# Opening with filler products, another order of transfers, block 1 plain; the last 24 modulation column tiles moved out of the raw ring

## The chip, the cores and the metric

The kernel runs on one core of one Trainium2 chip. The time is device microseconds (us) of that core for one launch. The kernel before takes 1838.76 us (median of 3 runs, 1837.59 to 1839.71). The engines are named PE (matrix products; PEld its weight loads), DVE (vector), ACT (scalar), POOL (GpSimd) and SP (the sync engine, which here issues most transfers). Each engine works through its own instructions strictly in order and waits at the first one that isn't ready.

## The reference

One layer of a diffusion trunk over 640 tokens: 512 latent ones, which use the conditioning vector `c`, and 128 context ones, which use `c_ctx`. The model width is 1024, the inner width of each FFN 2816. All is float32.

```python
def adaln(cvec, w, b):
    m = jax.nn.silu(cvec) @ w + b
    return m.reshape(cvec.shape[0], N_MOD, D_MODEL)        # N_MOD = 9

def swiglu(h, w1, w3, w2):
    return (jax.nn.silu(h @ w1) * (h @ w3)) @ w2

def layer(x, mods, l, p, ctx):
    m = [mods[:, j][:, None, :] for j in range(N_MOD)]
    hh = rmsnorm(x, g[0]) * (1 + m[1]) + m[0]
    x = x + 0.5 * m[2] * swiglu(hh, p['ffn1_w1'][l], p['ffn1_w3'][l], p['ffn1_w2'][l])
    hh = rmsnorm(x, g[1]) * (1 + m[4]) + m[3]
    y, ctx_out = token_mixer(hh, p, l, ctx)
    x = x + m[5] * y
    hh = rmsnorm(x, g[2]) * (1 + m[7]) + m[6]
    x = x + 0.5 * m[8] * swiglu(hh, p['ffn2_w1'][l], p['ffn2_w3'][l], p['ffn2_w2'][l])
```

`token_mixer` is a differential attention and an mLSTM side by side; its end is `y = sigmoid(gm) * (hm @ w_br_m) + sigmoid(gd) * (att @ w_br_d)` and then `y @ w_out`. The nine vectors `m[j]` depend on the conditioning alone: 9 x 1024 values for each of two vectors, which are 72 column tiles of 128 values.

## The kernel before

**Data.** The tokens lie along the free axis in two halves of 320 (`HALF`, `hf` 0 and 1), the features in 8 tiles of 128 partitions (`KT`). Every factor of a float32 product is split into a high and a low part, and a product is the three matmuls high x high, high x low and low x high (`mm3`), each 128x128 by 128x320. So a product of 128 outputs by 320 tokens over 1024 inputs takes 24 matmuls. All of them are recorded by one helper line (L75), and copies to the high part by L51 (ACT), differences to the low part by L54 (DVE), loads by L97. In the names, `wH` and `wL`, `ww`, `wB`, `wC` are split weights, `raw` the weights as loaded, `hm` and `S` the normalised activations and their sums.

**Stages.**

1. The opening (0 to about 53 us). `x` comes in by `load_x`; `Opening.squares`, `add_squares`, `rstd` and `refine` make the norm's 1/rms (the sum over partitions is a product with `ones`, tile `ps_ss`), `divide` applies it. The modulation columns m[0] and m[1] come from `Opening.product(k)`, 16 matmuls on a 1 MB piece of `w_ada` (`raw_a`, a ring of four buffers, `load(k)`), k = 0 to 7, and `columns(k)`, a small product (`ps_at`) after a copy on DVE (`small`, L802). `norm(hf, r)` applies scale and shift. Between these stand the eight steps of the first FFN block: `step(first, k, 0)` multiplies feature tile k of half 0. After them `second` does half 1. This stage is emitted in the order in which the code is written (`as_written`).
2. FFN1, up. The inner width is cut into 11 blocks of 256. Block 0 is the one of the opening, plain. From block 2 on, and for w3 of block 1, a block is done by Winograd's form: 7 products of 12 matmuls (84) in place of 4 of 24 (96) (`Winograd.products`), for which the weights' sums are made by `Granule.parts` and `sums` (`ww`, `wB`, `wC`; split on ACT, then on DVE). w1 of block 1 is plain (`Whole`). The step counter `i` runs over w1 and w3 of the blocks, two steps a block; `between(i, at)` puts other work into a step.
3. FFN1, down; the mixing (input projections, attention, mLSTM), with `Fill` granules put between.
4. The branches: products with `w_br_d` (tiles `w_brd`), with `w_br_m` (`w_brm`) and with `w_out`, 16 units each of 24 matmuls (`ps_p`); the sigmoid gates are read back from DRAM (`sig`), and `d_evac` and `m_evac` take the results out of PSUM on DVE.
5. FFN2, up and down (`HalfStep.run`): blocks 0 to 2 with their gate plain, 3 to 10 gated on Winograd's sums. The residual `x` is read again from `x2_dram` into `x_pairs`.

**Column tiles.** The other 56 column tiles are made by `Columns.tile` (L716): one tile is a load of 512 KB (`raw_a` or `ada`) and two DVE instructions, each of which multiplies it with one conditioning vector (`csil`) and sums. 14 of them stand in FFN1 up, 18 in FFN1 down, with loads on POOL's queue. The last 24 stand in the mixing and in stage 4. Their loads (`load_columns_raw`) share a ring of two buffers (`rawp`) with the weights `w_brd`, `w_brm`, `z_raw` and are issued by SP, in one queue with those.

**What sets the order.** Outside the parts emitted as written, a scheduler orders each engine's instructions; `tc.issue_after(x)` only says after which instruction the next ones may be put. Each engine's queue is in order, and so are SP's transfers: SP waits at a transfer until its buffer is free, and everything behind it waits too.

## Time and profile before

| | us |
|---|---|
| median of 3 runs | 1838.76 |
| the profiled execution | 1840.36 |
| its span in the profile | 1838.6 |
| PE busy in it | 1799.5 |
| DVE busy | 1317.2 |
| ACT busy | 867.7 |

The profiled execution is 1.6 us above the median. PE is busy for all but 39 us of the span. Busy does not mean full speed: its instructions also last longer where the granted clock is low, and the profile gives that clock for any stretch of time. The places at which PE waits, and what ended each wait, are listed with the prediction.

### The profile page before, as it was taken

The page shows a single profiled execution, that of the slowest core. Times are in us where ns is not written, and L with a number is a line of the kernel's source. Part 1 is how long each engine was busy: PE and PEld are TensorE (multiplying, and loading weights), DVE is VectorE, ACT ScalarE, POOL GpSimd, SP SyncE. Part 2 cuts the span into 40 slices and gives each one's busy share as a digit, 9 for nine tenths or more (in the row PEclk, how much of TensorE's full clock was granted, in tenths as well). Part 3 has the DMA queues.
Part 4 walks back from the last instruction along what each step waited for, and adds up shares of the span by engine and source line. Part 5 has one row for each costly group of instructions (what it writes and reads, how often), then busy time and mean ns, then how long its engine had stood idle before and what let it go on. Part 6 is the DMA issues. An engine that isn't in the chain of part 4 may idle for free.

```text
span 1838.6 us, 30679 instructions
## 1 busy us (share of the span) xinstructions
PE 1799.5 (98%) x12608; PEld 1761.4 (96%) x12608; DVE 1317.2 (72%) x2148; ACT 867.7 (47%) x1490; POOL 31.0 (2%) x55
## 2 busy tenths in 40 slices
PE   7999999999999999999999999999899999999999
PEld 5999999999999999999999999999899999999999
DVE  5898886577787757475585558876766878887575
ACT  4654454112655555454465555673235645554232
POOL 0000001110000000000000000000000000000000
PEclk8999999999999999999999999999999999999999
DMA  7354547975234322122222154574742345447872
GB/s 289 121 192 169 193 169 250 370 239 176 72 122 145 122 81 79 63 85 67 77 77 84 41 168 147 199 268 164 257 174 86 132 149 188 166 170 254 322 286 87
DMA packets 127709, 298.77 MB, mean 162 GB/s; under 512 B 9617, under 2 KB 90769, under 8 KB 114769
## 3 DMA queue, kind: packets, MB, share of 16 engines
q1 hardware_dynamic: 118306, 256.44, 40.1%
q0 software_dynamic: 9264, 40.37, 6.0%
q8 instruction: 99, 1.62, 0.4%
q14 instruction: 40, 0.33, 0.1%
HBM read 233.15 MB, written 63.63 MB: 161 GB/s over the span
## 4 chain that ended last, share of the span: by engine, by line
PE 84%; DVE 6%; DMA 5%; ACT 3%; issue 1%; SPq 0%; DVEq 0%; ACTq 0%
PE ps_f L75 45%; PE ps_p L75 16%; PE ps_t L75 11%; PE sc L75 3%; PE ps_o L75 2%; PE ps_n L75 2%; DMA ada<-csil_dram 2%; DVE ww L54 1%; PE ps_u L75 1%; PE ps_wT L78 1%; DMA raw_a<-in_w_ada_c 1%; PE ps_qkT L78 1%; DVE raw_a L716 1%; ACT wH L51 1%; PE ps_ss L75 1%
## 5 line engine op out<-in xcount | busy, mean ns | idle before, releaser
L75 PE MATMUL ps_f<-S,ww 128*128 128x320 f32 x2172 | 350.2, 310 | 5.8 <-DVE ww L54 4.2
L75 PEld LDWEIGHTS ps_f<-S,ww 128*128 128x128 f32 x2172 | 327.0, 189 | 8.5 <-DVE ww L54 6.9
L75 PE MATMUL ps_p<-hH,wH 128*128 128x320 f32 x672 | 213.4, 318 | 6.9 <-DVE y L54 6.2
L75 PE MATMUL ps_p<-hL,wH 128*128 128x320 f32 x672 | 208.2, 310 | 0.0
L75 PE MATMUL ps_p<-hH,wL 128*128 128x320 f32 x672 | 208.2, 310 | 0.0
L51 ACT ACTIVATE ww<-raw 128x2048 fp32r<-128x2048 f32 (+1 forms) x67 | 125.6, 1874 | 154.9 <-PE ps_f L75 87.6
L75 PE MATMUL ps_f<-hm,ww 128*128 128x320 f32 x1236 | 195.6, 311 | 2.5 <-DVE ww L54 2.5
L75 PEld LDWEIGHTS ps_f<-hm,ww 128*128 128x128 f32 x1236 | 185.8, 189 | 2.8 <-DVE ww L54 2.8
L75 PE MATMUL ps_t<-wH,hH 128*128 128x256 f32 x640 | 185.3, 289 | 0.9 <-DVE x L57 0.9
L75 PE MATMUL ps_t<-wH,hL 128*128 128x256 f32 x640 | 181.1, 283 | 0.9 <-DVE hL L54 0.9
L75 PE MATMUL ps_t<-wL,hH 128*128 128x256 f32 x640 | 180.9, 283 | 0.0
L54 DVE TENSOR_TENSOR ww<-raw,ww 128x2048 fp32r<-128x2048 f32 (+1 forms) x67 | 150.1, 2240 | 38.7 <-ACT ww L51 38.7
L75 PE MATMUL ps_f<-hm,wB 128*128 128x320 f32 x984 | 157.6, 309 | 0.0
L75 PEld LDWEIGHTS ps_f<-hm,wB 128*128 128x128 f32 x984 | 147.7, 188 | 0.0
L54 DVE TENSOR_TENSOR raw<-raw 128x1024 f32<-128x1024 f32 x159 | 137.6, 865 | 2.0
L75 PEld LDWEIGHTS ps_p<-hH,wH 128*128 128x128 f32 x672 | 126.9, 189 | 7.6 <-ACT wH L51 6.4
L75 PEld LDWEIGHTS ps_p<-hL,wH 128*128 128x128 f32 x672 | 126.9, 189 | 0.3
L75 PEld LDWEIGHTS ps_p<-hH,wL 128*128 128x128 f32 x672 | 126.7, 189 | 0.0
L54 DVE TENSOR_TENSOR wL<-raw,wH 128x2048 fp32r<-128x2048 f32 x43 | 98.3, 2286 | 35.6 <-ACT wH L51 35.6
L75 PEld LDWEIGHTS ps_t<-wH,hH 128*128 128x128 f32 x640 | 122.4, 191 | 1.5 <-ACT nsq L51 1.1
L75 PEld LDWEIGHTS ps_t<-wH,hL 128*128 128x128 f32 x640 | 122.4, 191 | 1.1 <-DVE hL L54 1.1
L75 PEld LDWEIGHTS ps_t<-wL,hH 128*128 128x128 f32 x640 | 122.5, 191 | 0.4
(303 smaller groups left out, 3353.7 us busy)
## 6 DMA issues: line engine op xcount, KB each, us to landing
g_dram<-g SPq DMA_DIRECT2D x44, 640.0 KB, 5.6
raw_a<-in_w_ada_c SPq DMA_DIRECT2D x24, 512.0 KB, 4.0
raw<-in_w1b SPq DMA_DIRECT2D x11, 1024.0 KB, 4.8
raw<-in_w3b SPq DMA_DIRECT2D x11, 1024.0 KB, 4.8
raw<-in_w1a SPq DMA_DIRECT2D x10, 1024.0 KB, 4.8
raw<-in_w3a SPq DMA_DIRECT2D x10, 1024.0 KB, 6.2
ada<-in_w_ada_c POOLq DMA_DIRECT2D x18, 512.0 KB, 5.0
hm<-g_dram POOLq DMA_DIRECT2D x7, 1280.0 KB, 10.5
```

Source lines behind the costliest of these rows:

```text
L51: return placed(nc.scalar.activation(*args, **kw))
L54: return placed(eng.tensor_tensor(out=out, in0=in0, in1=in1, op=op))
L75: tc.keep_in_program_order(nc.tensor.matmul(*args, **kw))
L78: tc.keep_in_program_order(nc.tensor.transpose(*args, **kw))
L716: placed(vec.tensor_tensor_reduce(out=junk, in0=raw, in1=self.csil[:, v, :], op0=ALU.mult, op1=ALU.add, scale=1.0, scalar=0.0, accum_out=m ...
```

## The change

- **Opening.** The transfer of `cT` goes from SP to ACT's queue, so that `x` is first on SP; the first piece of w1 and w3 (`load_weights(0)`) goes ahead of `raw_a` 0, the second half of `x` behind `raw_a` 5. New products of `ones` with `ones` (`keep_clock`, 128x128 by 128x128, tile `ps_idle`, read by nobody) stand in four places: 14 + 3 + 4 + 2. The squares of half 0 are added with three matmuls in place of two, after one addition of half the size; `rstd` stands ahead of `product(0)`, whose copy moves from DVE to ACT; `divide` works on one feature tile at a time for the first two. The squares of half 1 move to k = 3, their sum to k = 4, `refine(1)` from k = 5 to 6.
- **Block 1** of FFN1 is plain for w3 too (`whole_units` twice), so the Winograd form begins with block 2.
- **`products`**: the parts of the second granule are made ahead of `ahead()` (the second batch of operand sums), not behind it.
- **Column tiles.** 10 of the 24 stay in the mixing with the ring. 6 stand in stage 4 beside `w_br_m`, and 8 in FFN2 up at every second step (i = 3, 5, ..., 17). These 14 use one pair buffer for the load and one for `junk`, both of the residual's `x_pairs` (in FFN2 the other two hold `csil`, read again), and POOL's queue. So the second half of `x_pairs` is loaded behind the six tiles, and in FFN2 the residual is read again at step 18 instead of step 0, at which the pair buffers become free.

```diff
-    cT = load(cp, [128, KT, 2], a["cT"], name="cT")
+    cT = cp.tile([128, KT, 2], F32, name="cT")
...
+    nc.scalar.dma_start(out=cT, in_=a["cT"])
...
             if ahead is not None:
                 with tc.issue_after(work[0][0].split_at):
-                    behind = ahead()
+                    work[1][0].parts(self.fp)
+                with tc.issue_after(work[1][0].parts_at):
+                    ahead()
...
+            def keep_clock(self, n):
+
+                if not hasattr(self, "idle"):
+                    self.idle = self.bank(3, "ps_idle")
+                for _ in range(n):
+                    mm(self.idle[:, :128], ones, ones, start=True, stop=True)
...
-        for r in range(2):
-            start.squares(0, r)
-            start.add_squares(0, r)
+        start.keep_clock(14)
+        start.squares(0, 0)
+        start.add_squares(0, 0)
+        start.squares(0, 1)
+        split_weights(0, "high")
+        split_weights(0, "low", slice(1))
+        start.add_squares(0, 1)
+        start.rstd(0)
+        split_weights(0, "low", slice(1, 2))
         start.product(0)
         start.load(4)
-        load_weights(3)
-        start.rstd(0)
-        split_weights(0, "high")
+        load_weights(2)
+        start.keep_clock(3)
         start.refine(0)
         start.columns(0)
-        start.divide(0, 0)
+        start.keep_clock(4)
+        start.divide(0, 0, 1)
+        start.norm(0, 0)
         start.product(1)
-        split_weights(0, "low")
-        start.norm(0, 0)
+        start.divide(0, 0, 1, 1)
         start.load(5)
+        load_x(1, 0)
+        load_x(1, 1)
+        start.keep_clock(2)
...
+        whole_units(whole[0], gated[0], ((0, 1), (1, 1), (0, 0), (1, 0)))
         with tc.issue_after(end.ins), tc.issue_after(at_act.ins):
             third, fourth = hs.operand_sums(lambda r: x_all[:, 2 * r : 2 * r + 2, :])
+        whole[1].split()
+        hs.up[3].load()
+        hs.store_g(hs.SO, 0)
+        whole_units(whole[1], gated[1], ((0, 0), (1, 0), (0, 1), (1, 1)))
...
-    columns.place(24, csil2, load_columns_raw, 1)
+    columns.place(10, csil2, load_columns_raw, 1)
...
-        if i > 1:
-            columns.tile()
...
-    while fill.q:
-        fill.units(2)
-        if columns.n > 6:
-            columns.tile()
+    fill.drain()
...
+    def load_columns_pair(src):
+        raw = pair("k", 2, "raw_a").rearrange("p a t -> p (a t)")[:, :D]
+        nc.gpsimd.dma_start(out=raw, in_=src)
+        return raw, junk
...
+    columns.place(6, csil2, load_columns_pair, 1)
...
-        for g in range(4):
+        for g in range(2):
             nc.sync.dma_start(out=x_pairs[g], in_=x_dram[:, 2 * g : 2 * g + 2, :])
...
+                if not columns.n:
+                    x_pairs += [pair("k", i, "x") for i in range(2, 4)]
...
-    def after():
-        fourth()
-        for g in range(4):
-            nc.sync.dma_start(out=x_pairs[g], in_=x2_dram[:, 2 * g : 2 * g + 2, :])
-        hs.store_g(SO, 0)
+    def aside(i, at):
+        if (i, at) == (0, 1):
+            fourth()
+            hs.store_g(SO, 0)
+        elif (i, at) == (1, 1):
...
+            columns.place(8, Two(places[:2]), load_columns_pair, 1)
+        elif at and 3 <= i < 3 + 15 and i % 2 == 1:
+            columns.tile(hs.at_vec)
+        elif (i, at) == (18, 1):
+            x_pairs[:] = pairs("k", "x")
```

**Order, PE at the opening.** The first products of the program; `ps_idle` are the fillers, `ps_ss` the sums of squares, `ps_a` the products on `raw_a`, `ps_f` the first FFN block. One piece of the difference (`-` before, `+` the change):

```order
-L75 MATMUL ps_ss<-sq,ones 128x320 x4
+L75 MATMUL ps_idle<-ones 128x128 x14
+L75 MATMUL ps_ss<-sq,ones 128x320 x6
 L75 MATMUL ps_a<-raw_a,small 32x256 x8
+L75 MATMUL ps_idle<-ones 128x128 x3
 L75 MATMUL ps_at<-sel,small 128x2 x2
+L75 MATMUL ps_idle<-ones 128x128 x4
+L75 MATMUL ps_a<-raw_a,small 32x256 x8
+L75 MATMUL ps_idle<-ones 128x128 x2
+L75 MATMUL ps_f<-hm,wH 128x320 x4
+L75 MATMUL ps_at<-sel,small 128x2 x2
```

The fillers stand ahead of the sums of squares, around the first `ps_at`, and once more ahead of the first FFN step. `product(1)` now stands ahead of that step as before, and the second `ps_at` behind its first four products.

**Order, SP at the branches.** SP's queue where `w_br_d` ends and `w_br_m` begins. Before:

```order
L97 DMA z_raw<-zT_dram 128x1920
L97 DMA raw_a<-in_w_ada_c 128x1024
L97 DMA raw<-in_w_brd 128x2048
L97 DMA raw_a<-in_w_ada_c 128x1024 x4
L97 DMA raw<-in_w_brm 128x2048 x2
L2104 DMA x<-x_dram 128x1280 x4
```

and now:

```order
L97 DMA z_raw<-zT_dram 128x1920 x2
L97 DMA sig<-gd_dram 128x1280
L97 DMA raw<-in_w_brd 128x2048
L97 DMA raw<-in_w_brm 128x2048 x3
L2146 DMA x<-x_dram 128x1280 x2
```

The five `raw_a` ahead of the first `w_br_m` are gone from this queue, three of `w_br_m` stand right behind the last `w_br_d`, and two loads of `x` have moved behind.

**Order, DVE in FFN2 up, a step with a column tile** (w3 of a gated block). `SO`, `s`, `t` are gate work on the results, `ww`, `wC`, `wB` the split of the next granule's sums. Before:

```order
L54 TENSOR_TENSOR ww<-raw,ww 128x2048
L54 TENSOR_TENSOR s<-ps_f,u 128x320
L54 TENSOR_TENSOR wC<-raw,wC 128x512
L54 TENSOR_TENSOR SO<-ps_f,s 128x320
L54 TENSOR_TENSOR wB<-raw,wB 128x1024
L54 TENSOR_TENSOR t<-ps_f,u 128x320
```

and now:

```order
L54 TENSOR_TENSOR s<-ps_f,u 128x320
L54 TENSOR_TENSOR SO<-ps_f,s 128x320
L721 ISA junk,mod<-raw_a,csil 128x1024
L721 ISA mod 128x1
L54 TENSOR_TENSOR ww<-raw,ww 128x2048
L54 TENSOR_TENSOR wC<-raw,wC 128x512
L721 ISA junk,mod<-raw_a,csil 128x1024
L721 ISA mod 128x1
L54 TENSOR_TENSOR wB<-raw,wB 128x1024
```

The first half of the tile stands ahead of `ww`, the second between `wC` and `wB`. So it is in six of the eight tiles; in the other two `ww` and `wC` stand ahead of both halves.

More of the change, by code (lines that the diff above doesn't have):

```diff
@@ L401, in products @@
                     then[i + 2 - n].load()
-                if not last:
-                    with tc.issue_after(behind if i == 0 and ahead is not None else gr.split_at):
+                if not last and (i > 0 or ahead is None):
+                    with tc.issue_after(gr.split_at):
                         work[i + 1][0].parts(self.fp)
@@ L599, in run_whole, with run @@
                     unit(G[-1], j, f, 1)
-        def run(self, x, gate, final, ahead, after):
+        def run(self, x, gate, final, ahead, aside):
             def nothing(*args):
@@ L937, in tile_trunk @@
             if k == 5:
[L938 removed]
+                whole[0].split(t=[((0, 2048, w1[0]),), ((0, 1792, w1[1]), (1792, 2048, w1[2][:, :256]))])
                 hs.up[2].load()
```

112 lines of the change are left out of this document (70 added, 42 removed).

## The prediction

> **What bounds the kernel now.** I read the page first, then the waits of PE, then windows and timelines at the places where those waits lie.
>
> ```profile
> span 1838.6 us, 30679 instructions
> ...
> PE 1799.5 (98%) x12608; PEld 1761.4 (96%) x12608; DVE 1317.2 (72%) x2148; ACT 867.7 (47%) x1490; POOL 31.0 (2%) x55
> ```
>
> PE is the bound over the whole program: 39.1 us of the span are not busy. So a microsecond can come off only in three ways: fewer products, a wait of PE that goes, or products that run at a higher clock. The view of waits says what PE waited for:
>
> ```profile
> PE ps_ss L75 <- DVE sq L54: 7.7, 1, 7.7
> PE ps_f L75 <- DVE ww L54: 6.7, 7, 2.5
> PE ps_p L75 <- DVE y L54: 6.2, 1, 6.2
> PE ps_f L75 <- ACT hm L51: 2.7, 1, 2.7
> PE ps_at L75 <- DVE small L802: 2.2, 3, 1.1
> ```
>
> The columns are us in total, times, and the longest. These five rows are 25.5 of the 39.1 us, and the change touches the place of each: the opening (`ps_ss`, `hm`, `small`), the split weights `ww` at the start of each FFN, and the one wait of 6.2 in the branches.
>
> **The opening.** Windows (us, then each engine's busy time and count, then PE's granted clock, DMA share, GB/s):
>
> ```profile
> 15.40:19.20 3.80, 1.07 (x16) 0.42 (x16) 3.14 (x8) 2.19 (x5) 0.00 (x0) 0.73 1.03 388
> 19.20:31.20 12.00, 11.95 (x64) 9.23 (x64) 5.25 (x13) 4.94 (x8) 0.00 (x0) 0.52 1.04 404
> 33.70:38.00 4.30, 3.79 (x37) 2.74 (x40) 3.48 (x9) 2.99 (x6) 0.00 (x0) 1.00 0.67 271
> 38.00:42.00 4.00, 4.00 (x35) 3.10 (x35) 2.75 (x7) 1.71 (x3) 0.00 (x0) 1.00 0.00 2
> ```
>
> From 19.2 to 31.2 PE is busy throughout at a clock of 0.52: about 5.8 us of these 12 are lost to the clock. The transfers run full until 33.7 + 0.67 x 4.3 = 36.6 and then stop. The first FFN product waits for a chain; pieces of it (start, us), and then rows of PE's timeline:
>
> ```profile
> 0.74 0.40 SPq L97
> ...
> 6.79 0.83 DVE sq L54
> ...
> 12.30 1.77 PE ps_a L75 x16
> 14.10 0.42 DVE small L802
> ...
> 17.69 0.83 DVE x L54
> ```
> ```profile
> 19.25 1.44 PE L75 MATMUL ps_f<-hm,wH 128*128 128x320 f32 x4 [2.67 <-ACT hm L51]
> ...
> 39.83 0.99 PE L75 MATMUL ps_f<-hm,wH 128*128 128x320 f32 x4
> ...
> 42.36 1.07 PE L75 MATMUL ps_a<-raw_a,small 128*32 128x256 f32 x16
> 43.37 1.34 PE L75 MATMUL ps_ss<-sq,ones 128*128 128x320 f32 x4
> 44.30 0.99 PE L75 MATMUL ps_f<-hm,wH 128*128 128x320 f32 x4
> ...
> 46.84 1.07 PE L75 MATMUL ps_a<-raw_a,small 128*32 128x256 f32 x16
> ```
>
> What the edit takes from the chain: `x` no longer stands behind `cT` on SP (0.40); `rstd` no longer behind product 0 and its copy (from 12.30 to 14.52, 2.2); one addition and one division are half as long (0.4 each of 0.83). Together 3.4, so the first step stands at 15.8 instead of 19.25. If the clock is then full, a step costs 43.37 - 39.83 = 3.54 with its `ps_a`, and the sums of squares 44.30 - 43.37 = 0.93 a piece. The last product on `raw_a` (46.84) stands behind the first step's twelve products (42.36 - 39.83 = 2.53), five steps and two sums: 15.8 + 2.5 + 17.7 + 1.9 = 37.9, which is 8.9 less. Transfers give nearly the same floor: as many bytes as before go ahead of the last `raw_a`, so it lands near 37 again, a gain of at most 9.6. At full clock the copies on DVE have less room; `ps_at` waited 2.2 in three places already, and I add two waits of about half a microsecond (estimate from 2.2 over three). I take **-8.0**, between -3.4 (the chain alone, the clock as before) and -9.6. The 14 first fillers lie in the 7.7 us in which PE has nothing. The other 9 stand ahead of the first step; a product of 128 columns costs at most the 0.27 us of a 320-column one at low clock, so 2.4 us if that cover were gone; it is the 2.67 wait for `hm`. `cT` on ACT's queue holds ACT's first instruction until it lands; behind it are the squares, which need `x` anyway.
>
> A rule on the clock bears on this. The Trainium skill (TensorE: Matmul & The Clock Gate, What's actually happening) says the clock is halved by default, becomes full after about 3.4 us of sustained activity and falls back after an idle window. The fall after the wait of 2.67 us agrees with it, the 12 us at 0.52 with PE 11.95 busy do not; by the rule alone the fillers would hold the clock, by that row a single gap near the start would cost most of the 5.8 us.
>
> **Block 1 and the starts of the Winograd parts.** PE's timeline in FFN1 and in FFN2, and one window:
>
> ```profile
> 93.69 0.56 PE L75 MATMUL ps_f<-S,ww 128*128 128x320 f32 x2 [1.30 <-ACT ww L51]
> 96.02 3.04 PE L75 MATMUL ps_f<-S,ww 128*128 128x320 f32 x10 [1.77 <-DVE ww L54]
> ```
> ```profile
> 96.00:98.90 2.90, 2.88 (x11) 2.88 (x12) 2.90 (x4) 1.47 (x2) 0.00 (x0) 0.50 0.62 220
> ```
> ```profile
> 1462.02 1.92 PE L75 MATMUL ps_f<-hm,wC 128*128 128x320 f32 x12
> 1463.78 1.92 PE L75 MATMUL ps_f<-hm,wB 128*128 128x320 f32 x12
> ...
> 1470.83 1.73 PE L75 MATMUL ps_f<-S,ww 128*128 128x320 f32 x10 [1.32 <-DVE ww L54]
> ```
>
> Twelve products take 1463.78 - 1462.02 = 1.76 us at full clock (0.147 each). A plain w3 of block 1 has 96 instead of 84: +1.76. It covers the making of the first sums: both waits go (1.30 + 1.77 = 3.07), and with them the half clock behind them (2.90 x 0.50 = 1.45). Net **-2.7**; it is +1.8 if the same wait merely moves behind block 1, where the sums now have a whole plain step (96 x 0.147 = 14.1 us) more. In FFN2 the second granule's parts now precede the operand sums: the wait of 1.32 goes, **-1.3**, at worst 0.
>
> **The branches.** SP's queue, ACT's wait, PE's timeline, a window:
>
> ```profile
> 1270.85 16.96 SPq L97 DMA_DIRECT2D raw_a<-in_w_ada_c  x4
> 1290.17 3.94 SPq L97 DMA_DIRECT2D raw<-in_w_brm  x2
> ```
> ```profile
> ACT wH L51 <- DMA raw<-in_w_brm: 19.3, 2, 18.7
> ```
> ```profile
> 1280.67 0.41 PE L75 MATMUL ps_p<-aHL,wL 128*128 128x320 f32 x1 [1.08 <-DVE wL L54]
> ...
> 1300.90 0.60 PE L75 MATMUL ps_p<-hH,wH 128*128 128x320 f32 x1 [6.19 <-DVE y L54]
> ```
> ```profile
> 1300.90:1304.10 3.20, 3.20 (x12) 3.20 (x13) 2.05 (x1) 0.00 (x0) 0.00 (x0) 0.52 1.03 424
> ```
>
> The wait of 6.19 is put down to DVE's `y`, but DVE stood behind the split of `w_brm`, whose weights were late: SP spent 16.96 us on four `raw_a`, each waiting for a ring buffer that DVE had to free, and only at 1290.17 issued `w_brm`; ACT waited 18.7 for it. In the new order three `w_brm` follow `w_brd` directly, with the whole ring to themselves. So 6.19 goes, and the slow clock behind it (12 products in 3.20 instead of 1.76: 1.44). Of the 1.08 at the last `w_brd` I count 0.4, since that split keeps its place. **-8.0**, between -8.7 and 0. The six tiles in this stage cost PE nothing as long as DVE gets them done under 16 units of 24 products, 16 x 24 x 0.147 = 56.4 us; their price if not is the rival below.
>
> **The tiles in FFN2.** A tile in FFN1 and what PE's weight load waited behind it; DVE's load in FFN2; the transfers:
>
> ```profile
> 118.94 1.22 DVE L716 CUSTOM_DVE_ANT_0 junk<-raw_a,csil 128x1024 bf16<-128x1024 f32 x1
> ...
> 122.42 0.19 PEld L75 LDWEIGHTS ps_f<-S,ww 128*128 128x128 f32 x1 [0.38 <-DVE ww L54]
> ```
> ```profile
> 1500.00:1700.00 200.00, 200.00 (x1365) 200.00 (x1365) 159.97 (x202) 103.23 (x142) 0.00 (x0) 1.00 0.54 189
> ```
> ```profile
> raw_a<-in_w_ada_c SPq DMA_DIRECT2D x24, 512.0 KB, 4.0
> ...
> ada<-in_w_ada_c POOLq DMA_DIRECT2D x18, 512.0 KB, 5.0
> hm<-g_dram POOLq DMA_DIRECT2D x7, 1280.0 KB, 10.5
> ```
>
> PE has no gap in the 200 us, DVE is at 80%. Two steps last 2 x 84 x 0.147 = 24.7 us, of which DVE is busy 19.7; a tile adds 2 x 1.22 = 2.44, so it fits on average. But half a tile stands ahead of `ww` in six of the eight, as in FFN1, where PE then waited 0.38: 6 x 0.38, **+2.3**, between 0 and 8 x 2.44 = 19.5. A tile that waits for its load holds DVE, behind it `ww` and the gate work, and PE behind those; the load has two steps to land in, against 5.0. The re-reading of the residual (640 x 1024 floats, 2.6 MB) moves to the end of the up part; at 424 GB/s that is 6.2 us of transfers beside those with which the down part begins. I take **+0.5**, between 0 and 6.2. The eight loads stand on POOL ahead of the down part's `hm`, but the last is issued before step 17.
>
> **The sum.** -8.0 - 2.7 - 1.3 - 8.0 + 2.3 + 0.5 = -17.2. The profiled execution took 1840.36, so its like would take 1823.2; it lies 1.6 above the median 1838.76, from which the forecast is **1821.6**.
>
> **The rivals.**
>
> *The clock isn't held.* For it: 12 us at 0.52 with PE busy, after one gap of 2.67; the fillers are short and stand in four groups with gaps between. Against it: the gap is what they fill. Then the opening gives -3.4: 1821.6 + 4.6 = 1826.2.
>
> *The branch wait stays* (the change doesn't do what it says there). For it: the row names DVE's `y`, and `y` needs the gates' read-back `sig`, which keeps its place. Against: ACT's 18.7 ended with the landing of `w_brm`. Then +8.0: 1829.6.
>
> *DVE becomes the bound in FFN2.* Each tile delays PE by its whole length: 19.5 - 2.3 = 17.2 more, 1838.8, no change. For it: DVE's work is uneven, and `ww` is what PE waits for 7 times. Against: 2.5 us of each 24.7 are still free.
>
> *POOL's queue is too slow for one buffer* (slower). The six tiles in the branches share one load buffer, so a tile takes its landing time plus 2.44, and in the order the sixth stands on DVE ahead of the split of the first `w_out`. 56.4 / 6 - 2.44 = 7.0: up to a landing time of 7.0 us nothing is lost, beyond it six times the excess. With 5.0 there is room; with the 10.5 that `hm` took on the same queue, 6 x 3.5 = 21 and a slow clock of 1.4 behind: 1844.0. For it: the landing on POOL's queue is already 5.0 against 4.0. The Trainium skill (SBUF — State Buffer, SBUF: two separate sides) speaks for it as well: transfers issued by GpSimd have their descriptors written by it, and some DVE instructions lock it out meanwhile. By that rule the landing grows with DVE's load; the trace's 5.0 against 4.0, with DVE busy, is a small effect of that kind.
>
> **How the numbers follow.** The forecast 64%, the clock 16%, the branch wait 8%, DVE as the bound 5%, POOL's queue 7%. The first three lie between 1814 and 1832 with their own spread: at the low end all terms at their best (-9.6 - 2.7 - 1.3 - 8.7 = -22.3, 1816.5) and two more of the waits on `ww` (6.7 in all, 3.1 of them counted); at the high end the branch wait with 2 us of the other costs. I leave the last two out, so the range is **1814 to 1832**. About 0.2% (3.7 us) is what a measurement of this kernel tells from no change. Faster: the first three, 88%; within it: DVE as the bound, 5%; slower: POOL's queue, 7%.
>
> **What would show it.** Right: PE's first FFN step before 16.5 at a clock of 1.00 and the last `ps_a` near 38; no wait over 1 us between 85 and 105; no `ps_p` wait over 1 us in the branches; in FFN2 up six short waits on `ww`. Wrong: a clock near 0.5 after the first step (the first rival); a `ps_p` wait on `y` with `sig` late; waits on `ww` of 1 us and more at steps 3, 5, ..., 17; `raw_a` on POOL landing after 7 us and more with PE waiting at the first `w_out`.

## The result, and the profile after

The kernel with the change takes 1829.17 us (median of 4 runs, 1826.73 to 1829.58) against 1838.17 us for the kernel before on the same chip (4 runs, 1836.37 to 1839.71): a ratio of 0.9944, 95% interval 0.9932 to 0.9956. It is faster by about 9 us. The forecast, 1821.6, was 7.6 us too low. Of the changed kernel, the profiled execution took 1829.16 us. Its page:

```profile
span 1827.4 us, 30792 instructions
...
PE 1802.1 (99%) x12670; PEld 1764.7 (97%) x12670; DVE 1311.0 (72%) x2141; ACT 863.2 (47%) x1486; POOL 38.4 (2%) x69
```

The span fell by 11.2, and the time in which PE isn't busy from 39.1 to 25.3 (1827.4 - 1802.1). What PE waited for now (us in total, times, the longest):

```profile
PE ps_a L75 <- DMA raw_a<-in_w_ada_k: 3.7, 2, 1.9
PE ps_f L75 <- DVE ww L54: 3.6, 3, 3.3
PE ps_f L75 <- DMA hm<-g_dram: 2.2, 1, 2.2
...
PE ps_f L75 <- ACT u L51: 0.9, 1, 0.9
...
PE ps_p L75 <- DVE y L54: 0.7, 1, 0.7
```

All five rows that the prediction shows of before are gone or small: `ps_ss` 7.7, `hm` on ACT 2.7 and `small` 2.2 no longer stand among them, `y` fell from 6.2 to 0.7, and `ww` from seven waits to three. But one of those three is 3.3 long, and a transfer that PE never waited for, `hm<-g_dram`, now costs 2.2. Where each microsecond went is read from a few products that both programs have; here are their rows in PE's timeline (start, us). Before:

```profile
67.55 0.46 PE L75 MATMUL ps_f<-hm,wgA 128*128 128x320 f32 x2
393.40 1.92 PE L75 MATMUL ps_f<-op,ww 128*128 128x320 f32 x12
1235.88 0.46 PE L75 MATMUL ps_p<-aHL,wH 128*128 128x320 f32 x2
1379.80 0.31 PE L75 MATMUL ps_p<-hH,wo 128*128 128x320 f32 x1
1695.48 1.48 PE L75 MATMUL ps_f<-S,ww 128*128 128x320 f32 x9
1706.08 1.48 PE L75 MATMUL ps_f<-S,ww 128*128 128x320 f32 x9
```

and after:

```profile
60.35 0.46 PE L75 MATMUL ps_f<-hm,wgA 128*128 128x320 f32 x2
384.80 1.92 PE L75 MATMUL ps_f<-op,ww 128*128 128x320 f32 x12
1227.91 0.46 PE L75 MATMUL ps_p<-aHL,wH 128*128 128x320 f32 x2
1363.57 0.31 PE L75 MATMUL ps_p<-hH,wo 128*128 128x320 f32 x1
1680.08 1.48 PE L75 MATMUL ps_f<-S,ww 128*128 128x320 f32 x9
1694.61 1.48 PE L75 MATMUL ps_f<-S,ww 128*128 128x320 f32 x9
```

The difference of each pair is how far the changed program is ahead there; the difference of two such differences is what the stage between them gained (negative in the table) or lost.

| stretch, up to | ahead by | change of time in it | in the forecast |
|---|---|---|---|
| opening: first gate product | 7.20 | -7.20 | -8.0 |
| FFN1: products on `op` in its down part | 8.60 | -1.40 | -2.7 |
| mixing: first `w_brd` | 7.97 | +0.63 | 0 |
| branches: first `w_out` | 16.23 | -8.26 | -8.0 |
| FFN2 up: end, at the first `S` products of its down part | 15.40 | +0.83 | -1.3 + 2.3 = +1.0 |
| FFN2: start of the down part | 11.47 | +3.93 | +0.5 |

So the gain stood at 16.2 us at the first `w_out`, against 18.7 in the forecast up to there, and almost 5 us were given back in FFN2. These are differences of one execution each; how far a stage scatters is said where it matters.

**Opening.** Windows (us; busy time and count of PE, PEld, DVE, ACT, POOL; granted clock, DMA share, GB/s), then PE's timeline:

```profile
15.40:19.20 3.80, 3.80 (x39) 2.94 (x32) 2.28 (x6) 1.78 (x4) 0.00 (x0) 1.00 1.03 407
19.20:31.20 12.00, 12.00 (x119) 9.06 (x111) 8.17 (x20) 7.10 (x12) 0.00 (x0) 1.00 1.03 398
```
```profile
16.46 0.83 PE L75 MATMUL ps_f<-hm,wH 128*128 128x320 f32 x4
...
34.64 1.07 PE L75 MATMUL ps_a<-raw_a,small 128*32 128x256 f32 x16 [1.87 <-DMA raw_a<-in_w_ada_k]
...
40.19 1.07 PE L75 MATMUL ps_a<-raw_a,small 128*32 128x256 f32 x16
```

PE does 119 products in the 12 us in which it did 64 before: the clock is 1.00 and not 0.52. The first step starts at 16.46 (19.25 before) and the last `ps_a` at 40.19 (46.84). What stops PE now is the landing of `raw_a`.

**FFN1.** In its down part DVE has a column tile that needs `csil`, read back from `csil_dram`. This row of DVE, before, then the same instruction after, and what PE did behind it:

```profile
347.83 1.23 DVE L716 CUSTOM_DVE_ANT_0 ada<-ada 128x1024 bf16<-128x1024 f32 x1 [14.14 <-DMA ada<-csil_dram]
```
```profile
339.23 1.22 DVE L721 CUSTOM_DVE_ANT_0 ada<-ada 128x1024 bf16<-128x1024 f32 x1 [5.68 <-DMA ada<-csil_dram]
...
346.51 1.91 PE L75 MATMUL ps_f<-hm,ww 128*128 128x320 f32 x7 [3.31 <-DVE ww L54]
```

The two rows are 8.60 apart, exactly the offset of the `op` products behind them. DVE stood idle until `csil` landed, `ww` stood behind the tile, and PE waited 3.31 for `ww` (2.51 before): from here on the landing sets the time, and what was gained ahead of it beyond 8.60 is lost. SP began to issue this read-back (of the second conditioning vector) at 319.69 before and at 319.79 after, behind loads of `w2a`, though PE was 9.4 ahead there; the DMA share is 1.03 and 1.04 from 320 to 340 us, so the transfers were full in both. Why it landed 8.60 earlier all the same isn't shown.

**Branches.** The first row is of PE's timeline, the second a window, the third a row of the view of transfers for 1280 to 1370 us (KB each, median us from issue to landing):

```profile
1286.06 0.38 PE L75 MATMUL ps_p<-hH,wH 128*128 128x320 f32 x1 [0.68 <-DVE y L54]
```
```profile
1284.00:1364.00 80.00, 79.33 (x541) 79.10 (x540) 56.76 (x93) 27.93 (x33) 2.67 (x6) 1.00 0.58 206
```
```profile
raw_a<-in_w_ada_c POOLq DMA_DIRECT2D x6, 512.0 KB, 5.1
```

The wait of 6.19 is 0.68, the clock behind it is 1.00, and the loads on POOL's queue land after 5.1 us, well below the 7.0 from which, by the prediction's estimate, the tiles would have held the stage up.

**The start of FFN2's down part.** PE's timeline, a window around it, and SP's queue ahead of it, in the kernel before and now:

```profile
1687.70 2.24 PE L75 MATMUL ps_f<-hm,ww 128*128 128x320 f32 x9 [2.17 <-DMA hm<-g_dram]
```
```profile
1685.00:1692.00 7.00, 4.83 (x23) 4.56 (x22) 1.92 (x4) 0.00 (x0) 0.00 (x0) 0.76 1.02 413
```
```profile
1683.04 2.59 SPq L615 DMA_DIRECT2D S<-g_dram  x2
1686.96 1.04 SPq L97 DMA_DIRECT2D raw<-in_w2b  x2
1688.63 1.72 SPq L615 DMA_DIRECT2D hm<-g_dram  x1
```
```profile
1664.43 0.52 SPq L618 DMA_DIRECT2D hm<-g_dram  x1
...
1665.85 1.50 SPq L97 DMA_DIRECT2D raw<-in_w2b  x2
...
1668.16 2.04 SPq L618 DMA_DIRECT2D S<-g_dram  x1
...
1672.48 3.49 SPq L97 DMA_DIRECT2D raw<-in_w2b  x2
1676.06 1.29 SPq L618 DMA_DIRECT2D hm<-g_dram  x1
```

The up part stores its results `g` and reads them back as the operands `hm`, `S`, `S`, `hm` of the down part, all on SP, and the loads of `w2b` stand between them. The last read-back is issued at 1676.06, behind two `w2b` that took the queue 3.49 us. PE waits 2.17 for it, and the clock falls behind the wait (0.76 over these 7 us). Before, both `S` were through and the two `w2b` took 1.04, and PE didn't wait. The fall of the clock doesn't come in every execution: in experiments 3 and 4, with the same program here, PE waits 1.88 and 2.00 and the clock stays at 1.00. The stretch between the two last markers of the table (1680.08 to 1694.61, 14.53 us) takes them 12.70 and 12.83, and the kernel before 10.60.

### The profile page after: what moved, and what is told of

The parts are those of the page before. It is cut to its first block, busy times and chain, and to the rows that moved or that the text cites. A ratio compares the mean times of both kernels' runs of the same rounds, so it can differ in the third digit from the quotient of the medians.

```text
span 1827.4 us, 30792 instructions
## 1 busy us (share of the span) xinstructions
PE 1802.1 (99%) x12670; PEld 1764.7 (97%) x12670; DVE 1311.0 (72%) x2141; ACT 863.2 (47%) x1486; POOL 38.4 (2%) x69
## 3 DMA queue, kind: packets, MB, share of 16 engines
q8 instruction: 99, 1.62, 0.4%
## 4 chain that ended last, share of the span: by engine, by line
PE 86%; DVE 6%; DMA 4%; ACT 2%; issue 1%; SPq 0%; DVEq 0%; ACTq 0%
PE ps_f L75 44%; PE ps_p L75 19%; PE ps_t L75 11%; PE sc L75 3%; PE ps_o L75 2%; PE ps_n L75 2%; DVE ww L54 2%; DMA raw_a<-in_w_ada_k 1%; PE ps_u L75 1%; PE ps_wT L78 1%; DMA ada<-csil_dram 1%; DVE junk L721 1%; PE ps_qkT L78 1%; DMA hm<-g_dram 1%; DMA csil<-in_c_rows 0%
## 5 line engine op out<-in xcount | busy, mean ns | idle before, releaser
L75 PE MATMUL ps_f<-S,ww 128*128 128x320 f32 x2136 | 345.9, 311 | 2.6 <-ACT u L51 0.9
L75 PEld LDWEIGHTS ps_f<-S,ww 128*128 128x128 f32 x2136 | 321.9, 189 | 6.7 <-DVE ww L54 5.4
L75 PE MATMUL ps_p<-hH,wH 128*128 128x320 f32 x672 | 212.6, 316 | 1.7 <-DVE stage L61 0.7
L75 PE MATMUL ps_f<-hm,ww 128*128 128x320 f32 x1320 | 208.2, 311 | 5.5 <-DVE ww L54 3.3
L75 PE MATMUL ps_p<-hH,wL 128*128 128x320 f32 x672 | 207.7, 309 | 0.0
L75 PE MATMUL ps_p<-hL,wH 128*128 128x320 f32 x672 | 207.6, 309 | 0.0
L75 PEld LDWEIGHTS ps_f<-hm,ww 128*128 128x128 f32 x1320 | 198.1, 189 | 6.0 <-DVE ww L54 3.6
L75 PE MATMUL ps_t<-wH,hH 128*128 128x256 f32 x640 | 185.2, 289 | 0.9 <-DVE x L57 0.9
L54 DVE TENSOR_TENSOR ww<-raw,ww 128x2048 fp32r<-128x2048 f32 (+1 forms) x67 | 150.1, 2240 | 48.5 <-ACT ww L51 48.5
L75 PE MATMUL ps_t<-wH,hL 128*128 128x256 f32 x640 | 181.1, 283 | 0.9 <-DVE hL L54 0.9
L75 PE MATMUL ps_t<-wL,hH 128*128 128x256 f32 x640 | 180.9, 283 | 0.0
L75 PE MATMUL ps_f<-hm,wB 128*128 128x320 f32 x960 | 153.8, 309 | 0.0
L75 PEld LDWEIGHTS ps_f<-hm,wB 128*128 128x128 f32 x960 | 144.1, 188 | 0.0
L54 DVE TENSOR_TENSOR raw<-raw 128x1024 f32<-128x1024 f32 x156 | 134.7, 863 | 1.8
L75 PEld LDWEIGHTS ps_p<-hH,wH 128*128 128x128 f32 x672 | 126.3, 188 | 2.8 <-issue 0.9
L75 PEld LDWEIGHTS ps_p<-hL,wH 128*128 128x128 f32 x672 | 126.3, 188 | 0.3
L75 PEld LDWEIGHTS ps_p<-hH,wL 128*128 128x128 f32 x672 | 126.1, 188 | 0.0
L75 PEld LDWEIGHTS ps_t<-wH,hH 128*128 128x128 f32 x640 | 122.4, 191 | 1.5 <-ACT nsq L51 1.1
L54 DVE TENSOR_TENSOR wL<-raw,wH 128x2048 fp32r<-128x2048 f32 x43 | 98.3, 2286 | 35.5 <-ACT wH L51 35.3
L75 PEld LDWEIGHTS ps_t<-wH,hL 128*128 128x128 f32 x640 | 122.4, 191 | 1.1 <-DVE hL L54 1.1
L75 PEld LDWEIGHTS ps_t<-wL,hH 128*128 128x128 f32 x640 | 122.6, 192 | 0.4
```

The costliest lines, as they stand in the source:

```text
L54: return placed(eng.tensor_tensor(out=out, in0=in0, in1=in1, op=op))
L75: tc.keep_in_program_order(nc.tensor.matmul(*args, **kw))
```

## The experiments

All of them compute the whole output. Each is the changed kernel with the edit shown, except one that is the kernel before with fillers. Ratios are to the kernel before on the same chip, with 95% intervals; the changed kernel's own is 0.9944 [0.9932, 0.9956]. Times in single traces are of one profiled execution of each kernel.

**1. No fillers.** Is it the `ps_idle` products that hold the clock in the opening?

```diff
             def keep_clock(self, n):
+                return
```

> The changed kernel without the 23 filler products; all else of its opening stays. If the fillers hold the clock: PE's granted clock falls to about 0.5 again for some 10 us behind the first step, the last product on raw_a, at 40.19 in the changed kernel, stands 3 to 5 us later, and the time is 3 to 5 us longer (1832 to 1834). If the new order alone holds the clock (PE busy early enough without them): no change. If the landing of raw_a is what sets the opening whatever the clock is: the clock falls, but the last product on raw_a moves by less than 1 us.

1828.98 us, ratio 0.9931 [0.9913, 0.9949]: no loss. The window of the opening, in this kernel:

```profile
19.20:31.20 12.00, 12.00 (x117) 8.81 (x116) 7.87 (x20) 7.66 (x13) 0.00 (x0) 1.00 1.04 402
```

The clock is 1.00 without fillers, and the first gate product stands at 60.01 (60.35 with them). PE's gaps from 11 to 19 us are then 0.3 to 0.7 us each, none of 2.67. The mean granted clock of the four runs is 0.996 to 0.999, as in the changed kernel. So the new order is enough, and the fillers bring nothing on top of it. Which part of the order does it (`rstd` earlier, a copy off DVE, `x` first on SP) isn't told apart.

**2. The fillers alone, in the kernel before.** Nine of them into the gap of 2.67 us.

```diff
         start.product(1)
+        start.keep_clock(9)
         split_weights(0, "low")
```

> The kernel before with nothing but nine filler products in the gap of 2.67 us ahead of its first FFN step. If that gap is what halves the clock from 19.2 to 31.2: the granted clock stays at 1.00 there, the first step stays near 19.25, the last product on raw_a comes 4 to 6 us sooner than 46.84 (no sooner than 40, where the loads let it in the changed kernel), and the time is 4 to 6 us below the kernel before. If the clock there depends on something else (what the products are, or time since the start): it is half all the same, no change. The second says also that the order alone, not the fillers, gave the changed kernel its opening.

In its profiled execution the second of these windows has the full clock too, and the first gate product comes 4.6 us earlier (62.93):

```profile
15.40:19.20 3.80, 3.80 (x30) 2.78 (x23) 3.73 (x9) 1.79 (x3) 0.00 (x0) 0.59 1.03 387
19.20:31.20 12.00, 11.44 (x107) 8.94 (x105) 8.03 (x20) 6.54 (x11) 0.00 (x0) 1.00 1.04 405
```

But the first window shows that the clock fell all the same, and ahead of the fillers: they start at 16.71, and the clock is 0.55 from 15 to 16 us already, behind these products and a gap of 0.83:

```profile
14.94 1.84 PE L75 MATMUL ps_a<-raw_a,small 128*32 128x256 f32 x16 [0.83 <-DMA raw_a<-in_w_ada_k]
```

In the kernel before it falls in the gap (0.58 from 17 to 18) and comes back between 30 and 31; here it comes back between 18 and 19. Worked out from the shares of these windows, it was low for some 13.6 us before and some 3.4 here. So the gap of 2.67 isn't shown to be what closes the clock; it may be what kept it low for so long, which one pair of executions can't show.

The ten runs have a median of 1837.64, ratio 0.9997 [0.9984, 1.0009]: no gain. The profiled execution is the fastest of the ten (1834.74), and that of the kernel before lies 1.6 above its median. The mean granted clock of the ten is 0.992 to 0.997, and 0.992 to 0.996 in the thirteen runs of the kernel before beside them. So the 4.6 us of this pair don't stand for the two kernels, and what sets the clock here stays open. The Trainium skill (TensorE: Matmul & The Clock Gate, What's actually happening) gives about 3.4 us of activity until the clock is full; the 3.4 us of this execution agree with it, before's 12 us at 0.52 with PE 11.95 busy don't, and no run here shows why.

**3. The second half of `x` behind one more load.** The opening now waits for `raw_a`; here two of its competitors go later.

```diff
-        load_x(1, 0)
-        load_x(1, 1)
...
                 if k == 0:
+                    load_x(1, 0)
+                    load_x(1, 1)
                     load_weights(3)
-            if k == 3:
+            if k == 4:
...
-            if k == 4:
+            if k == 5:
```

> The changed kernel with the second half of x read behind raw_a 6 instead of ahead of it, and its squares and sums one step later. If the loads now bound the opening (the wait of 1.87 us on raw_a 6 at 34.64): this wait goes, the last product on raw_a stands at 38.3 instead of 40.19, and the time is 1 to 2 us shorter, 1827.5. If the chain of the second half's norm then ends last (x, squares, sums, rstd, divide): the second block waits for hm by as much, no change.

1829.47 us, ratio 0.9948 [0.9933, 0.9963]: nothing gained. The wait of 1.87 at 34.64 goes to the next load:

```profile
38.42 1.07 PE L75 MATMUL ps_a<-raw_a,small 128*32 128x256 f32 x16 [2.44 <-DMA raw_a<-in_w_ada_k]
```

and though the last `ps_a` is 1.8 us earlier, the first gate product is at 61.16, 0.8 later: PE then waits 0.86 for `hm` of the second half at 46.38 (0.60 at 45.58 in the changed kernel). The changed kernel and the eight others with just its opening have their first gate product at 59.85 to 61.75, so the 0.8 may be scatter; a gain isn't seen. Whether the opening is at the floor that its transfers set isn't shown by this.

**4. Block 1 in the Winograd form again for w3.**

```diff
-        whole = [Whole(4, gr.fetch) for gr in hs.up[:2]]
...
+        whole = [Whole(4, hs.up[0].fetch)]
...
-        whole_units(whole[1], gated[1], ((0, 0), (1, 0), (0, 1), (1, 1)))
```

> The changed kernel with w3 of block 1 in the Winograd form again, as before. From the account (two waits of 3.1 us in all and 1.4 us of half clock behind them, against twelve products, 1.76 us): the waits on ww come back right behind block 1's w1 and the stage from the first block's gate to the down part is 2.7 us longer; the time 1831.9. The rival, that these waits moved with the clock or the opening and not with block 1: no wait of over 1 us there, and the time falls by the 1.8 us of the saved products.

1831.8 us (6 runs), ratio 0.9962 [0.9947, 0.9977], some 3 us above the changed kernel by the ratios, with intervals that still overlap. PE's timeline has two waits again, one of them on the sums `S`:

```profile
84.18 2.82 PE L75 MATMUL ps_f<-S,ww 128*128 128x320 f32 x11 [1.77 <-DVE S L54]
...
103.67 1.74 PE L75 MATMUL ps_f<-S,ww 128*128 128x320 f32 x10 [1.70 <-DVE ww L54]
```

At the end of FFN1's up part this kernel is 3.4 us behind the changed one. In its profiled execution it catches up where `csil` lands: the wait there is 1.23 instead of 3.31, and the clock behind it 1.00 from 345 to 350 us instead of 0.69. So the landing, with the clock behind it, swallows what the changed kernel had gained ahead of it. This execution falls behind again in the mixing (158.58 us against 155.43), where the two programs are the same. So the two waits are shown to be block 1's, but the 3 us of the medians are not.

**5. FFN1's column tiles behind the landing of `csil`.** So I moved the tiles to steps behind it.

```diff
-                columns.tile(hs.at_vec)
-                if at and i in (20, 22):
+                if i > 20:
                     columns.tile(hs.at_vec)
+                    if at and i < 25:
+                        columns.tile(hs.at_vec)
```

> The changed kernel with the 18 column tiles of FFN1 down beginning one step later (two a half step then). The wait at its start (3.31 us in the changed kernel, 2.51 before, and a half clock behind it, 1.5 to 1.7) stands behind a tile on DVE that waits for the reading of csil. If that tile is what holds ww: the wait goes, 4 to 5 us shorter, 1824.7. If ww is late because its weights are (the loads of w2a): the wait stays, no change, or moves to the next split.

1824.13 us, ratio 0.9916 [0.9899, 0.9932]: 5.0 us below the changed kernel. The row of 3.6 us on `ww` in the view of waits is now

```profile
PE ps_f L75 <- DVE ww L54: 0.6, 4, 0.2
```

and FFN1, from the first gate product to `op`, takes 319.26 instead of 324.45 us. That stage scatters between executions even where its program is the same: 321.4 to 325.3 in the seven kernels here with the changed kernel's FFN1, and 318.9 to 319.6 in the four with the tiles moved (experiments 5, 10, 11 and 12). The two groups don't overlap, so its own gain is 2 to 6 us.

**6. All 24 tiles back in the mixing with the ring, none in FFN2.** The residual is again read at step 0 of FFN2.

```diff
-    columns.place(10, csil2, load_columns_raw, 1)
+    columns.place(24, csil2, load_columns_raw, 1)
...
+        if i > 1:
+            columns.tile()
...
+        if columns.n > 6:
+            columns.tile()
...
-        elif at and 3 <= i < 3 + 15 and i % 2 == 1:
-            columns.tile(hs.at_vec)
```

> The changed kernel with the last 24 column tiles back where they were (the raw ring in the mixing and the branches, none in FFN2, the residual read at step 0 of FFN2). From the account of the two traces the move gave 8.2 in the branches and took 2.3 in FFN2 up, 3.9 at the start of FFN2 down and 0.6 in the mixing, so undoing it costs about 1.4 us net: 1830.6, with the wait of about 6 us at the first product on w_brm back and no wait on hm in FFN2 down. The rival, that the wait in the branches went for another reason (the gates' read-back): no such wait comes back and the time falls by about 6 us, to 1823.

1832.07 us, ratio 0.9951 [0.9937, 0.9966]. The view of waits has the branches' waits back, and no `hm<-g_dram`:

```profile
PE ps_p L75 <- DVE y L54: 6.2, 1, 6.2
...
PE ps_p L75 <- DVE wL L54: 1.6, 1, 1.6
```

At the end of FFN2's up part SP's queue has the read-backs in an order in which the last one is kept up less:

```profile
1672.14 2.62 SPq L618 DMA_DIRECT2D S<-g_dram  x2
1676.08 1.28 SPq L97 DMA_DIRECT2D raw<-in_w2b  x2
1677.76 1.95 SPq L618 DMA_DIRECT2D hm<-g_dram  x1
```

Two `w2b` stand ahead of it here too, but take the queue 1.28 us and not 3.49, and both `S` are through before them. The branches take 145.19 us instead of 135.66 (143.92 before). They take 135.66 or 135.67 in all ten kernels that have the 14 tiles moved, and 143.06 to 145.19 in the four with all 24 in the ring. FFN2's up part, to its last `hm,wC` products, takes 273.13 instead of 275.39, and from there to the first `op` products 51.14 instead of 55.01. So moving the tiles gains 9.5 in the branches and gives back 2.3 + 3.9 in FFN2: its net worth is about 3 us, and the ratios, 0.9944 and 0.9951, don't tell even that apart.

**7. FFN2's tiles behind the split of the next weights.** If a tile costs because it stands ahead of `ww`, it should cost nothing behind it.

```diff
-            columns.tile(hs.at_vec)
+            with tc.issue_after(hs.run_steps[i + 1][0].split_at):
+                columns.tile()
```

> The changed kernel with each of the eight tiles of FFN2 up put behind the split ww of its step on DVE; steps and buffers stay, and SP's queue keeps its order at the end of the up part (the second pair of w2 loads behind the first read-back of hm). If a tile costs PE because it stands ahead of ww: the 2.3 us of FFN2 up go. If the loss at the start of the down part comes from the last ww being late (so that the raw buffer is free late): it goes too, together 5 to 6 us, 1823.5. If it comes from the place of the second pair in SP's queue, or from the bytes of the re-reading: it stays at about 3.9, together 2.3, 1827.

1834.66 us, ratio 0.9971 [0.9958, 0.9985]: about 5 us worse. Four waits like this one of PE's timeline stand in FFN2 up:

```profile
1540.18 1.73 PE L75 MATMUL ps_f<-S,ww 128*128 128x320 f32 x10 [1.64 <-DVE ww L54]
```

FFN2 up takes 280.73 instead of 275.39. A reading that isn't tested: the tile then pushes the gate work and the sums behind it, and a later `ww` is late by more. The place chosen in the change is the better one.

**8. The last tile at step 15 instead of 17.** Does the tile nearest to the end make the down part late?

```diff
-        elif at and 3 <= i < 3 + 15 and i % 2 == 1:
+        elif at and i in (3, 4, 5, 7, 9, 11, 13, 15):
```

> The changed kernel with the eight column tiles of FFN2 up at steps 3, 4, 5, 7, 9, 11, 13, 15 in place of 3, 5, ..., 17. The scheduler then puts the reading of the residual two steps earlier and the second pair of w2 loads ahead of the first read-back of hm. If the loss of 3.9 us at the start of FFN2 down comes from the last tile and the re-reading standing there: the wait of 2.17 on hm goes, the time is 3 to 4 us shorter (1825.5). If it comes from something else of the down part (the bytes that it needs itself): the wait stays, no change.

1825.83 us, ratio 0.9921 [0.9906, 0.9935]; the wait on `hm` falls from 2.17 to 1.17. The clock stays at 1.00 behind it, and the stretch that takes 14.53 us in the changed kernel takes 11.99. It helps, but the wait doesn't go.

**9. The re-reading of the residual, late, without tiles.** Experiment 6 with the four transfers of the residual held back to step 17.

```diff
+        elif (i, at) == (17, 1):
+            with tc.issue_after(hs.at_vec.ins):
+                x_pairs[:] = pairs("k", "x")
+                for g in range(4):
+                    vec.memset(x_pairs[g][:, 0, 0:1], 0.0)
+                    nc.sync.dma_start(out=x_pairs[g], in_=x2_dram[:, 2 * g : 2 * g + 2, :])
```

> The changed kernel with the columns back in the ring (as in the run with all 24 there: no tile in FFN2), and only the re-reading of the residual at the end of FFN2 up, between the two pairs of w2 loads, behind four small writes that hold it there. If the bytes of the re-reading make the loss of 3.9 us at the start of the down part: a wait on hm of 2 us and more appears, 1836. If the lateness of the last ww (from the column tiles on DVE), which frees the buffer of the second pair, makes it: no wait on hm, 1832 as without the re-reading.

1831.79 us (8 runs), ratio 0.9964 [0.9948, 0.9981], and PE doesn't wait for `hm` in FFN2's down part. The four transfers are issued 24.0 us ahead of the last `hm,wC` products, and 24.9 to 21.0 ahead in the changed kernel. So the bytes of the residual, from which the forecast had its bound of 6.2, are not the cause.

**10. Experiments 5 and 8 together.**

```diff
+                if i > 20:
                     columns.tile(hs.at_vec)
...
+        elif at and i in (3, 4, 5, 7, 9, 11, 13, 15):
```

> Two edits together: the tiles of FFN2 up by step 15, and those of FFN1 down beginning one step later. If each gives what its own account says, they add up: 3 from the first and 4 to 5 from the second, 1821.5, a ratio to before of 0.990. If they share a cause or the denser tiles of FFN1 down make new waits: no better than the first alone, 1826.

1822.42 us, ratio 0.9904 [0.9888, 0.9921]. It is 6.8 us below the changed kernel, against 5.0 and 3.3 for the two alone, so most of both stays; so does a wait of 1.01 on `hm`.

**11. Experiments 3 and 5, and the last tile at step 13.** Now no tile is near the end, and four loads of `w2b` stand ahead of the first read-back; two more still stand ahead of the last one and take the queue 2.97 us.

```diff
+        elif at and i in (3, 4, 5, 6, 7, 9, 11, 13):
```

> Three edits together: x behind raw_a 6, FFN1 down's tiles one step later, FFN2 up's tiles at steps 3, 4, 5, 6, 7, 9, 11, 13, so that in SP's queue all four w2 loads stand ahead of the down part's read-backs again. If the lateness of the second w2 pair makes the rest of the wait on hm (1.0 us with the last tile at step 15): that wait goes; against the run with both tile edits (1822.4) 1.4 us from there and 0 to 2 from the opening, 1820. If four tiles in a row crowd DVE: waits on ww of over 1 us at steps 4 to 8, 1824 and more.

1829.6 us (1823.92 to 1830.51), ratio 0.9942 [0.992, 0.9964]: a miss. The wait on `hm` isn't smaller but larger, 2.73, and the tiles in a row at the start hold `ww` up by 2.30. So the nearness of the last tile alone doesn't make the wait.

**12. The read-backs on another queue.** Experiment 5, with only the queue of the four read-backs changed from SP to POOL; tiles, `w2b` and residual stay where they are.

```diff
-... A11: lambda: fetch(0, 0), S1: lambda: fetch(0, 1), S2: lambda: fetch(0, 2), A12: lambda: fetch(0, 3) ...
+... A11: lambda: fetch(0, 0, nc.gpsimd), S1: lambda: fetch(0, 1, nc.gpsimd), S2: lambda: fetch(0, 2, nc.gpsimd), A12: lambda: fetch(0, 3, nc.gpsimd) ...
```

> The changed kernel with FFN1 down's tiles one step later, and in FFN2 only the four read-backs of g for the first down group (hm, S, S, hm) on POOL's queue in place of SP's; the last column tile (step 17), the late ww and the re-reading of the residual stay where they are. If the loss at the start of FFN2 down comes from SP's in-order queue (read-backs that wait for PE and stores that wait for DVE hold up one another and the second fetch of hm): the wait on hm of 2 us goes though tile and bytes stay, and the time is 3 to 4 us below the run with the later FFN1 tiles alone (1824.1): 1820.5. If the bytes in that stretch, or the lateness of DVE itself, make the loss: the wait stays at about 2 us, 1824.

1821.98 us, ratio 0.9912 [0.9897, 0.9927]. PE doesn't wait for `hm`, and the clock over the start of the down part is 1.00. The four read-backs in POOL's timeline:

```profile
1659.94 0.72 POOL L618 DMA_DIRECT2D hm<-g_dram  x1 [34.66 <-PE ps_f L75]
...
1661.70 0.73 POOL L618 DMA_DIRECT2D S<-g_dram  x1 [1.04 <-PE ps_f L75]
...
1665.23 0.70 POOL L618 DMA_DIRECT2D S<-g_dram  x1 [2.79 <-PE ps_f L75]
...
1668.74 0.72 POOL L618 DMA_DIRECT2D hm<-g_dram  x1 [2.81 <-PE ps_f L75]
```

Each is released by PE's products, and none stands behind a load of `w2b`. The times of experiments 5 and 12 alone would not tell them apart (0.7 us by the ratios, 2.2 by the medians, and their intervals overlap); the wait that is gone from the profile does. Nine kernels in one table, with the issue of the last read-back against the start of the last `hm,wC` products of the up part (negative is earlier):

| kernel | last read-back issued | PE's wait on `hm` |
|---|---|---|
| 6 and 9, no tiles in FFN2 | -2.01 | 0 |
| 12, read-backs on POOL | -1.74 | 0 |
| 8, last tile at 15 | -1.12 | 1.17 |
| 10 | -1.07 | 1.01 |
| 5 | +0.61 | 1.98 |
| changed kernel | +0.82 | 2.17 |
| 7, tiles behind the split | +1.26 | 2.72 |
| 11, last tile at 13 | +1.62 | 2.73 |

Experiments 1, 3 and 4, with the changed kernel's FFN2, fit in: +0.03 to +0.12, with waits of 1.88 to 2.01. The wait follows the time at which the read-back is issued, whatever else differs: in all nine kernels that wait, the wait ends 11.5 to 12.6 us behind the issue, and PE needs `hm` 10.1 us behind the start of those products. So it comes late because it is issued late. Why it takes some 12 us isn't told apart; the DMA share is 1.02 in the window above. The Trainium skill (DMA: Bandwidth & Descriptors, Issuing engines are not separate DMA queues) says that issuing transfers from several engines saves only the time to issue them; here it saved a wait of 1.98 us, on a queue on which nothing stood ahead of the read-backs that had to wait.

Experiments 10 and 12 are the fastest kernels here, both faster than the one before and the changed one; the intervals of the two overlap.

## Why the prediction was right and wrong

The sign, the place of the gain, and the range were right; the forecast was 7.6 us too low. Of this, 1.6 is the step from the profiled execution to the median: before's profiled execution lay 1.6 above its median and I took that off, but after's lies at its median. The other 6.0 are terms of the sum (-17.2 against -11.2 measured):

- **Opening: -8.0 forecast, -7.20 measured.** The order of events came as worked out: no wait for `hm` ahead of the first step, full clock, first step at 16.46 where I had 15.8 (and "before 16.5"), last `ps_a` at 40.19 where I had 37.9; 1.87 of these 2.3 are PE's wait on `raw_a`. That the clock was full is right, but not by the means that I named: I took the fillers for what holds it, and experiment 1 shows full clock without them, so that part of the term is partly luck. The missing 0.8 is no more than the scatter of the first gate product (59.85 to 61.75 over the kernels with this opening). The bound of -9.6 is a slip of 0.2 (46.84 to "near 37" is 9.8) and changes nothing.
- **Block 1: -2.7 forecast, -1.40 measured for the whole of FFN1.** The waits of 1.30 and 1.77 and the half clock behind them are gone; a wait of 0.88 on ACT's `u` is new. The two executions are 9.41 apart at the end of the up part (products on `hm,ww` at 322.23 and 312.82) and 8.60 behind the landing of `csil`. So the up part brought 2.21, near this term, and what was missing is a term: I didn't ask what stands next in the program and waits for something other than PE. It is a tile on DVE that waits for `csil`, whose wait of 14.14 before was in the trace. Experiment 5 moved the tiles behind it and the kernel became 5.0 us faster.
- **Mixing: 0 forecast, +0.63.** No experiment is about it; from the `ps_k` products to the first `w_brd` it took 154.88 us before, 155.67 in experiment 2 with before's program, and 155.15 to 158.6 in kernels with the changed one, so this may be scatter.
- **Branches: -8.0 forecast, -8.26 measured.** Right, with its mechanism: experiment 6 undoes it and the 6.2 come back. The landing on POOL's queue, 5.1, stayed under the 7.0 from which that rival began.
- **FFN2 up: +1.0 forecast, +0.83 measured.** The start wait of 1.32 is gone; the tiles cost 2.15 where I took 6 x 0.38 = 2.3 from a tile in FFN1. PE's weight load has just these six waits in FFN2, by its view of waits from 1400 to 1690 us (`PEld ps_f L75 <- DVE ww L54: 2.3, 6, 0.4`). Experiment 6 without tiles agrees: 2.3 less. The rival in which DVE becomes the bound would have cost 17 more.
- **Start of FFN2's down part: +0.5 forecast, +3.93 measured.** This is the step that failed, 3.4 of the 6.0. "I take +0.5, between 0 and 6.2" priced the bytes of the residual. The value lies inside those bounds, but for another reason: experiment 9 moves the same bytes and PE waits for nothing. By experiment 12 and the table, it is SP's queue: the read-backs of `g` and the loads of `w2b` now stand mixed, the last read-back comes 2.8 us later against PE's products than without the tiles, and PE waits 2.17. The rest is the clock behind the wait, which by experiments 3 and 4 falls in some executions only, so some 1.7 us of this loss are not sure to come. I had looked at POOL's queue, to which transfers were added, and not at SP's, in which the order of these had changed.

These come to 0.80 + 1.30 + 0.63 - 0.26 - 0.17 + 3.43 = 5.73; the remaining 0.27 lies behind the start of the down part.

Of the rivals, the clock not held fell (1.00 from 15.4 to 31.2 us), the branch wait fell, DVE as the bound fell, and POOL's queue fell. The change was worth less for reasons that none of them named, above all the order in SP's queue.

## What to carry to other kernels

When work is moved away from a stage, look for the next thing that doesn't move with the gain: an instruction on an in-order engine that waits for a transfer can swallow part of what was gained ahead of it. When tiles go into a stage, price not only the engine that does them but the order that they leave in each queue behind; a read-back that PE will need soon is better on a queue on which nothing waits ahead of it. And test a remedy by itself: the changed kernel is as fast without its fillers.

## What the runs showed of the hardware that was not expected

- In the opening the granted clock fell behind different gaps and stayed low for different times: in the kernel before in a gap of 2.67 us, for some 13.6 us, though PE was busy for 11.95 of the 12 us from 19.2; in experiment 2 behind gaps of 0.55 and 0.83 us, for some 3.4. In experiment 1, with gaps of 0.3 to 0.7 us in the same place, it stayed at 1.00; so it did in the changed kernel behind a gap of 1.78 (before the `ps_a` at 11.79). No run here shows the rule.
- Moving four issues from SP's queue to POOL's took away a wait of 1.98 us of PE though they move the same bytes, and POOL's loads landed after 5.1 us with DVE busy for 56.76 of 80 us.
- Behind waits of PE of the same length at the start of FFN2's down part the clock fell in some executions (2.17 and 2.01: 0.76 and 0.80 over 7 us) and not in others (2.00 and 1.88: 1.00).
- One and the same stretch of program (FFN1 from the first gate product to `op`) took from 321.4 to 325.3 us in seven kernels, so a single profile can't tell an edit of 2 us there from scatter.
